# Local attention in a hybrid decoder layer: two halves of a block's values stored unadded, and summed by an adding load from GpSimd's queue

## The chip, the cores and the metric

The kernel runs on one NeuronCore of one Trainium2 chip. The metric is the device time of one execution in microseconds (us); lower is better. The engines are named as the profile names them: PE (TensorE, matrix products; PEld is its weight loads), DVE (VectorE), ACT (ScalarE), POOL (GpSimd) and SP (SyncE, which here only issues DMAs). Each engine executes its own instructions in the order in which they stand; semaphores hold an instruction back until what it needs is done. DMAs are moved by 16 DMA engines that all queues share.

## The reference

One layer of a decoder takes 1024 prompt tokens and 8 single-token samples through the same weights. A combined projection feeds three branches (a gated recurrence, a local attention, an attention over a memory); each is projected, gated and summed, then follow an output projection, a layer norm, a gated feed-forward and a second layer norm. What the change touches is the local attention of the prompt, in blocks of 128 tokens with a window of 128, 16 query heads in groups of 4 per key/value head, and the product of its output with the second branch weight:

```python
def swa_prompt(q, k, v, sinks):
    ...
    s = jnp.einsum('bnqkgd,bnmkd->bnkgqm', qb, kband).astype(jnp.float32) * scale
    ...
    p = sink_softmax(s, mask, sinks).astype(v.dtype)
    o = jnp.einsum('bnkgqm,bnmkd->bnqkgd', p, vband)
    return o.reshape(B, T, Q_W)
...
    merged = sum(gates[:, :, n] * (br @ w_branch[n]) for n, br in enumerate((a_out, s_out, c_out)))
    h = layer_norm(ALPHA * x + merged @ w_out, ln1_g, ln1_b)
```

All is float32. The kernel gets this precision from faster products by splitting an operand into a rounded part ("hi") and the rest ("lo"): three products, hi by hi, hi by lo and lo by hi, stand for one.

## The kernel before

The 1032 columns (1024 prompt tokens and 8 samples) are worked on in three chunks of 388, 386 and 258 (`CH`). Activations pass from stage to stage through buffers in DRAM, `scr_*`. The branches are projected in the order a, c, s (recurrence, memory, local attention). The products of a and c are "fill": a generator `jobs`, of which `fill(n)` takes n products of 24 matmuls each, so that PE has dense work while the attention's softmax runs on the other engines. The tile framework makes dependencies, places buffers and orders the instructions of each engine by its own estimates from the program's order, so an edit can move neighbours too.

**The window phase** (`windows`) runs over 4 key/value heads by 8 blocks, 32 in all. For each block `win_scores` makes scores on PE, adds the mask and takes a minimum on DVE, exponentiates on ACT, and normalises on DVE, POOL and ACT. One block later `win_values` transposes the probabilities on PE (tile `bt`), splits them (`bph` is rounded by ACT on L80, `bpl` is the rest by DVE on L81), and multiplies them by the values on PE (L613 and L614) into one bank `bo` of PSUM, 128 partitions by 512 columns. The values carry their own hi and lo part side by side in the 128 stationary columns, so partitions 0 to 63 of `bo` hold the product of one part, 64 to 127 that of the other, and the block's output is their sum. L616 to L622 make it, in two pieces of 256 columns: ACT copies partitions 64 to 127 to SBUF (L618, tile `bob`), DVE adds partitions 0 to 63 (L619), and SP stores the sum to `scr_s` (L621). `bob` has four buffers, two blocks' worth.

**The load of branch s** follows at once: `load_branch("s", 0)` before the last two fill products are finished, and chunks 1 and 2 inside `branch(2, "s")`. For each chunk and each of 8 rows k (128 channels each), SP loads the columns from `scr_s` into the tile `bsL` (L135), ACT rounds it into `bsH` and DVE subtracts it from `bsL` in place (L80, L81). For branch a's first two chunks the same line issues from POOL's queue. The products of branch s then come in the order m=0, m=1 for chunk 0, the same for chunks 1 and 2, and then m=2 to 7 (L114 to L116, tile `brs`). Each takes all 8 rows of its chunk in the order of k. DVE gates and sums the result (L652, L653, gate tile `gts`, loaded by SP on L669).

Of the kernel before, what the change touches and what calls it, by code (L numbers as in the profile page):

```python
# [10 lines left out]
F32 = mybir.dt.float32  # L11
F32R = mybir.dt.float32r
AF = mybir.ActivationFunctionType
ALU = mybir.AluOpType
# [4 lines left out]
P = 128  # L19
D = 1024  # L20
KT = D // P
TP = 1024
NB = 8
T = TP + NB
# [33 lines left out]
class Builder:  # L58
# [66 lines left out]
    def load_branch(self, br, c):  # L125

        act = self.act.setdefault(br, [[None] * 3 for _ in range(KT)])
        t0, n = CH[c]
        for k in range(KT):
            if br == "s":  # L130
                hi, lo = (self.slot(e, c, f"b{br}{e}{k}_{c}", 0) for e in "HL")
            else:
                hi, lo = self.hl(k, t0, n)
            queue = self.nc.gpsimd if br == "a" and c < 2 else self.nc.sync
            queue.dma_start(lo.bitcast(F32), self.scr[br][:, k, t0:t0 + n])  # L135
            self.split(hi, lo, lo.bitcast(F32))
            act[k][c] = (hi, lo)

# [462 lines left out]
    def win_values(self, kv, ops, b, pg):  # L601
        nc = self.nc
        nk, vs = len(range(max(b - 1, 0), b + 1)), ops[2]
        ov = self.bank("o", f"bo{kv}_{b}")
        for kk in range(nk):
            pt = self.bank("t", f"bt{kv}_{b}_{kk}")
            for g in range(4):
                nc.tensor.transpose(pt[:, g * P:(g + 1) * P], pg[g][:, kk * P:(kk + 1) * P], self.ident)
            hi = self.ph.tile([P, 512], F32R, tag="pt", name=f"bph{kv}_{b}_{kk}", bufs=4)
            lo = self.ph.tile([P, 512], F32R, tag="pt", name=f"bpl{kv}_{b}_{kk}", bufs=4)  # L610
            self.split(hi, lo, pt)
            v = vs[:, max(b - 1, 0) + kk, :]
            nc.tensor.matmul(ov, v, hi, start=kk == 0, stop=False)  # L613
            self.last_mm = nc.tensor.matmul(ov, v, lo, start=False, stop=kk == nk - 1).ins  # L614
        for i in range(2):
            ob = self.ph.tile([64, 256], F32, tag="ob", name=f"bob{kv}_{b}_{i}", bufs=4)  # L616
            o = ov[:, i * 256:(i + 1) * 256]
            nc.scalar.copy(ob, o[64:128, :])  # L618
            nc.vector.tensor_add(ob, o[0:64, :], ob)  # L619
            dst = self.scr["s"][:, 2 * kv + i, b * P:(b + 1) * P].rearrange("(e d) t -> d e t", e=2)  # L620
            nc.sync.dma_start(dst, ob.rearrange("p (e t) -> p e t", e=2))  # L621

    def windows(self, fill):

# [674 lines left out]
    def build(self):  # L1299
        nc, tc, io = self.nc, self.tc, self.io  # L1300
        self.setup()
        self.sums = 3
        self.sm = self.ctx.enter_context(tc.tile_pool(name="sm", bufs=4))
        shapes = {"c": [P, KT, T], "s": [P, KT, T], "a": [P, KT, T], "g": [P, 24, T], "xq": [P, KT, 2, TP],
                  "q": [P, KT, 2, TP], "k": [P, 2, 2, TP], "v": [P, 8, 512]}
        self.scr = {b: self.dram.tile(n, F32, name=f"scr_{b}") for b, n in shapes.items()}
        self.scf = [self.dram.tile([P, T], F32, name=f"scr_f{f}") for f in range(NF)]
        self.cdec = self.cst.tile([P, KT, NB], F32, name="cdec")
        pool = lambda name, side="left": tc.tile_pool(name=name, bufs=1, side=side, reuse_waits="tile")
        self.wpool = self.ctx.enter_context(pool("wpool"))  # L1310
        self.ctx.enter_context(pool("edge", "right")).tile([P, 8], F32, name="edge")
        with pool("tp", "right") as self.tp, pool("w1") as self.w1, pool("z") as self.z, pool("dp1") as self.dp:
            self.project()
        self.sums = 2
        self.act, self.merged = {}, [[None] * 3 for _ in range(KT)]
        with pool("acc") as self.acc:
            with pool("slots0", "right") as slots0:
                hy = ExitStack()
                tails = [hy.enter_context(pool("hy")), slots0]
                cut = CH[2][0]  # L1320
                self.HL = [([slots0.tile([P, cut], F32R, name=f"HL{k}{e}") for e in "hl"],
                            [tails[k // 4].tile([P, T - cut], F32R, name=f"HT{k}{e}") for e in "hl"]) for k in reversed(range(KT))][::-1]
                self.M = [self.acc.tile([P, T], F32, tag="acc", name=f"M{m}", bufs=8) for m in range(KT)]
                with ExitStack() as gp:
                    self.gp = gp.enter_context(pool("gp"))
                    jobs = chain(self.branch(0, "a"), self.branch(1, "c"))

                    def fill(n):
                        for _ in range(n):
                            next(jobs, None)  # L1330

                    with pool("ph1") as self.ph, pool("dp2") as self.dp:
                        self.mem_attention(fill)
                    with pool("ph2") as self.ph:
                        self.windows(fill)
                    late = ExitStack()
                    self.slots = [late.enter_context(pool("slots1", "right"))]
                    self.load_branch("s", 0)
                    fill(4)
                    for _ in self.branch(2, "s"):  # L1340
                        pass
                with pool("ph5") as self.ph:
                    self.out_proj(self.merged)
                    late.close()
                    self.tp = late.enter_context(pool("tp2", "right"))
                    self.w1 = late.enter_context(pool("ea", "right"))
                    direct = self.direct_units()
                    next(direct)
                with pool("cb") as self.cb:
                    next(direct)  # L1350
                    self.h_sums(1)
                    next(direct)
                    self.h_sums(2)
                    next(direct)
                    units = self.units()
                    next(units)
                    self.h_sums(6)
                hy.close()
                with pool("w2") as self.w2:
                    next(units)  # L1360
                late.close()
            with pool("ph6") as self.ph, pool("gd", "right") as self.gd:
                self.down()
# [146 lines left out]
```

## Time and profile before

| | |
|---|---|
| median of three runs | 1955.13 us (1952.33 to 1958.13) |
| the profiled execution | 1952.96 us, of which the span of the program is 1951.2 us |
| mean granted TensorE clock | 0.997 of full speed |
| window phase | about 840 to 1040 us of the span |
| load and first products of branch s | about 1041 to 1069 us |

Times in the profile are counted from the start of the span. In a row of groups stand the line, the engine, the operation, the tiles (output, arrow, inputs), the shape and the count; then the busy time, the mean of one instruction, and the idle time of the engine just ahead of them with what ended it. A tile's answer gives durations as minimum, median and maximum in ns. In a row of stretches, x is a count of instructions, PEclk the granted clock, and the DMA share the mean busy share of the 16 DMA engines (it can pass 1 a little, since packets overlap).

### The profile page before, as it was taken

The numbers are of one execution on the slowest core, as the hardware profiler recorded it, in microseconds if no ns is written. First come the engines' busy times: TensorE is split into PE (matmuls) and PEld (weight loads), VectorE is DVE, ScalarE is ACT, GpSimd is POOL, SyncE is SP. The second block draws the span as 40 slices with busy tenths as digits, with TensorE's granted clock in tenths as the row PEclk, the third lists the DMA queues.
The fourth block names the chain that finished last, engine by engine and source line by source line (L and its number), as shares of the span: only waits on it lengthen the run. The fifth ranks groups of instructions, "written<-read, shape, count | busy, mean of one in ns | idle before, by whom it ended". The sixth has DMA issues, their size and how long they took to land. (4 is left out here: it accounts for less than half of the span.)

```text
span 1951.2 us, 37943 instructions
## 1 busy us (share of the span) xinstructions
PE 1916.7 (98%) x14356; PEld 1887.1 (97%) x14356; DVE 1365.5 (70%) x2875; ACT 1015.2 (52%) x2198; POOL 139.3 (7%) x218
## 2 busy tenths in 40 slices
PE   8999999999999999999999999999999999999997
PEld 8999999999999999989999999999999999999997
DVE  8678987888777555389877557975565655747566
ACT  5455565456556446288775245643333333635445
POOL 1000000000011200011210000000000000402001
PEclk9999999999999999999999999999999999999999
DMA  7444555365323867567525241123222222846554
GB/s 231 149 163 151 169 170 180 126 207 171 130 90 135 278 212 226 153 173 210 163 74 176 94 145 43 47 71 98 77 87 87 88 82 73 284 127 187 154 155 143
DMA packets 170919, 281.92 MB, mean 144 GB/s; under 512 B 20864, under 2 KB 85456, under 8 KB 170704
## 3 DMA queue, kind: packets, MB, share of 16 engines
q1 hardware_dynamic: 165840, 264.70, 43.3%
q0 software_dynamic: 4896, 14.80, 2.3%
q8 instruction: 112, 1.84, 0.4%
q14 instruction: 71, 0.58, 0.1%
HBM read 214.64 MB, written 66.85 MB: 144 GB/s over the span
## 5 line engine op out<-in xcount | busy, mean ns | idle before, releaser
L1238 PE MATMUL dl<-gh,wd_l 128*128 128x388 f32 (+2 forms) x528 | 168.9, 321 | 2.1 <-DVE wd_l L81 2.1
L1236 PE MATMUL dl<-gh,wd_h 128*128 128x388 f32 (+2 forms) x528 | 168.8, 320 | 1.1 <-ACT gh L80 1.1
L1237 PE MATMUL dl<-gl,wd_h 128*128 128x388 f32 (+2 forms) x528 | 168.3, 319 | 0.0
L1238 PEld LDWEIGHTS dl<-gh,wd_l 128*128 128x128 f32 x528 | 99.5, 189 | 2.6 <-DVE wd_l L81 2.6
L1236 PEld LDWEIGHTS dl<-gh,wd_h 128*128 128x128 f32 x528 | 99.5, 189 | 1.3 <-ACT gh L80 1.3
L1237 PEld LDWEIGHTS dl<-gl,wd_h 128*128 128x128 f32 x528 | 99.8, 189 | 0.5 <-DVE gl L81 0.5
L1245 POOL DMA_DIRECT2D gl<-scr_f x66 | 35.5, 538 | 794.4 <-PE fb L1172 635.9
L80 ACT CAST u_1h<-us 128x512 fp32r<-128x512 f32 x48 | 29.8, 621 | 88.4 <-issue 43.5
L591 ACT ACTIVATE bp<-bp,bst 128x257 f32<-128x257 f32 (+1 forms) x128 | 62.7, 493 | 17.5 <-DVE bst L587 17.4
L80 ACT CAST u_2h<-us 128x512 fp32r<-128x512 f32 x48 | 29.7, 619 | 76.7 <-PE fb L1171 38.1
L283 DVE TENSOR_TENSOR us<-ur,ur 128x512 f32<-128x512 f32 x96 | 66.1, 688 | 4.2 <-DMA ur<-win 1.8
L283 DVE TENSOR_TENSOR us<-us,ur 128x512 f32<-128x512 f32 x96 | 66.3, 690 | 2.3
L81 DVE TENSOR_TENSOR u_6l<-ur,u_6h 128x512 fp32r<-128x512 f32 x48 | 33.8, 704 | 43.7 <-PE fb L1172 27.1
L114 PE MATMUL brs<-bsH,wbs_h 128*128 128x388 f32 (+2 forms) x192 | 61.4, 320 | 1.0 <-ACT bsH L80 1.0
L115 PE MATMUL brs<-bsL,wbs_h 128*128 128x388 f32 (+2 forms) x192 | 61.6, 321 | 0.0
L116 PE MATMUL brs<-bsH,wbs_l 128*128 128x388 f32 (+2 forms) x192 | 61.6, 321 | 0.0
L81 DVE TENSOR_TENSOR u_4l<-us,u_4h 128x512 fp32r<-128x512 f32 x48 | 33.1, 689 | 40.5 <-PE fb L1172 29.2
L587 DVE CUSTOM_DVE_ANT_0 bp<-bs,mask,nsnk 128x256 f32<-128x256 f32 (+1 forms) x128 | 54.5, 458 | 2.9 <-PE bs L584 2.2
L81 DVE TENSOR_TENSOR u_5l<-us,u_5h 128x512 fp32r<-128x512 f32 x48 | 33.1, 690 | 30.4 <-PE fd L1172 14.8
L1190 ACT ACTIVATE ft<-za 128x516 f32<-128x516 f32 x40 | 25.5, 637 | 52.3 <-DVE za L1189 52.3
L80 ACT CAST u_0h<-ur 128x512 fp32r<-128x512 f32 x48 | 29.8, 621 | 38.5 <-PE ub L300 20.6
L80 ACT CAST u_5h<-us 128x512 fp32r<-128x512 f32 x48 | 29.9, 623 | 38.2 <-DVE us L283 23.4
(2762 smaller groups left out, 8117.6 us busy)
## 6 DMA issues: line engine op xcount, KB each, us to landing
ur<-win SPq DMA_DIRECT2D x112, 256.0 KB
ur<-wgu SPq DMA_DIRECT2D x80, 256.0 KB
scr_f<-ft SPq DMA_DIRECT2D x40, 258.0 KB
dck<-cmk SPq DMA_DIRECT2D x32, 256.0 KB
dcv<-cmvT SPq DMA_DIRECT2D x32, 256.0 KB
st<-scr_q SPq DMA_DIRECT2D x32, 256.0 KB
scr_g<-za SPq DMA_DIRECT2D x10, 516.0 KB
scr_g<-zb SPq DMA_DIRECT2D x10, 516.0 KB
```

Of the source, the lines that this page charges most:

```text
L80: ins = self.nc.scalar.copy(hi, src).ins
L81: self.nc.vector.tensor_sub(lo, src, hi.bitcast(F32))
L114: nc.tensor.matmul(ps, sh, mh, start=i == 0, stop=False)
L115: nc.tensor.matmul(ps, sh, ml, start=False, stop=False)
L116: self.last_mm = nc.tensor.matmul(ps, sl, mh, start=False, stop=closes and i == last).ins
L283: nc.vector.tensor_add(src, a, b)
L587: nc.vector.tensor_tensor_reduce(pg[g], s[:, u * 256:u * 256 + n], msk, 1.0, snk[:, g:g + 1], ALU.add, ALU.min, st[:, g:g + 1])
L591: nc.scalar.activation(x, x, AF.Exp, bias=st[:, g:g + 1], scale=-1.0, accum_out=st[:, 4 + g:5 + g])
L1236: nc.tensor.matmul(ps, sh, mh, start=k == 0, stop=False)
L1237: nc.tensor.matmul(ps, sh, ml, start=False, stop=False)
L1238: self.last_mm = nc.tensor.matmul(ps, sl, mh, start=False, stop=closes and k == NF - 1).ins
L1245: self.nc.gpsimd.dma_start(lo.bitcast(F32), self.scf[f][:, t0:t0 + n])
```

## The change

The two halves are no longer added on DVE. ACT copies the whole bank `bo` at once, 128 partitions by 512 columns, and SP stores it in four pieces: partitions 0 to 63 to `scr_s`, 64 to 127 to a new DRAM buffer `scr_s2`. When branch s is loaded, a second DMA on POOL's queue reads the same columns of `scr_s2` and adds them to what stands in `bsL`. It covers the 1024 prompt columns; the 8 sample columns are in `scr_s` alone, so in the last chunk it takes 250 of 258.

```diff
@@ load_branch
             queue.dma_start(lo.bitcast(F32), self.scr[br][:, k, t0:t0 + n])
+            if br == "s":
+                held = min(n, TP - t0)
+                self.nc.gpsimd.dma_start(lo[:, :held].bitcast(F32), self.scr["s2"][:, k, t0:t0 + held],
+                                         accum_op=ALU.add)
             self.split(hi, lo, lo.bitcast(F32))
@@ win_values
-        for i in range(2):
-            ob = self.ph.tile([64, 256], F32, tag="ob", name=f"bob{kv}_{b}_{i}", bufs=4)
-            o = ov[:, i * 256:(i + 1) * 256]
-            nc.scalar.copy(ob, o[64:128, :])
-            nc.vector.tensor_add(ob, o[0:64, :], ob)
-            dst = self.scr["s"][:, 2 * kv + i, b * P:(b + 1) * P].rearrange("(e d) t -> d e t", e=2)
-            nc.sync.dma_start(dst, ob.rearrange("p (e t) -> p e t", e=2))
+        ob = self.ph.tile([P, 512], F32, tag="ob", name=f"bob{kv}_{b}", bufs=2)
+        nc.scalar.copy(ob, ov)
+        for e in range(2):
+            for i in range(2):
+                dst = self.scr["s" if e == 0 else "s2"][:, 2 * kv + i, b * P:(b + 1) * P]
+                nc.sync.dma_start(dst.rearrange("(e d) t -> d e t", e=2),
+                                  ob[64 * e:64 * e + 64, 256 * i:256 * i + 256].rearrange("p (e t) -> p e t", e=2))
@@ build
-        shapes = {"c": [P, KT, T], "s": [P, KT, T], "a": [P, KT, T], "g": [P, 24, T], "xq": [P, KT, 2, TP],
+        shapes = {"c": [P, KT, T], "s": [P, KT, T], "s2": [P, KT, TP], "a": [P, KT, T], "g": [P, 24, T], "xq": [P, KT, 2, TP],
```

The built programs show where the instructions stand. Lines of the change are four higher from `load_branch` on (L138 is the adding load, L620 the copy, L624 the store, L656 and L657 are L652 and L653 of before). First SP's queue at the end of the window phase, before: the stores of the last block and the loads of chunk 0.

```order
L621 DMA scr_s_73<-bob3_7_0_14001 64x2x128
L621 DMA scr_s_73<-bob3_7_1_14005 64x2x128
L135 DMA bsL0_0_14014<-scr_s_73 128x388
L135 DMA bsL1_0_14019<-scr_s_73 128x388
L135 DMA bsL2_0_14024<-scr_s_73 128x388
L135 DMA bsL3_0_14029<-scr_s_73 128x388
```

The same place of SP's queue in the change, as far as the gate and the first load of chunk 1:

```order
L624 DMA scr_s_73<-bob3_7_13940 64x2x128 x2
L624 DMA scr_s2_74<-bob3_7_13940 64x2x128 x2
L135 DMA bsL0_0_13951<-scr_s_73 128x388
L135 DMA bsL1_0_13957<-scr_s_73 128x388
L135 DMA bsL7_0_13993<-scr_s_73 128x388
L673 DMA gts1_14095<-scr_g_76 128x1032
L135 DMA bsL0_1_14139<-scr_s_73 128x386
```

Between `bsL1_0` and `bsL7_0` stand rows 2 to 6 of the same kind. Two stores of the last block have become four; the loads behind them keep their order.

Second, POOL's queue in the change at the same place (before, nothing stands on POOL between its last normalisation of the window phase and the loads of the last stage, which begin at 1663.1 us of the span):

```order
L602 TENSOR_SCALAR bp3_6_13713<-bp3_6_13713,bst3_6_13712 128x256
L602 TENSOR_SCALAR bp3_7_13795<-bp3_7_13795,bst3_7_13794 128x256
L138 DMA bsL0_0_13951<-scr_s2_74 128x388
L138 DMA bsL1_0_13957<-scr_s2_74 128x388
L138 DMA bsL2_0_13963<-scr_s2_74 128x388
L138 DMA bsL0_1_14139<-scr_s2_74 128x386
L138 DMA bsL0_2_14245<-scr_s2_74 128x250
```

All 24 adding loads stand there in the order of chunk and row (the rows between are alike). Each waits for the plain load of its tile.

Third, DVE at the start of branch s, before: the last products of branch c are gated, then the first operands are split.

```order
L652 SCALAR_TENSOR_TENSOR gtc7_13937<-gtc7_13937,brc7_2_14080 128x258
L81 TENSOR_TENSOR wbs11_l_14161<-wbs1r1__14158,wbs11_h_14160 128x512
L81 TENSOR_TENSOR bsL0_0_14014<-bsL0_0_14014,bsH0_0_14013 128x388
L81 TENSOR_TENSOR bsL1_0_14019<-bsL1_0_14019,bsH1_0_14018 128x388
L653 TENSOR_TENSOR M7_8972<-M7_8972,gtc7_13937 128x258
```

And in the change:

```order
L656 SCALAR_TENSOR_TENSOR gtc7_13876<-gtc7_13876,brc7_2_14025 128x258
L81 TENSOR_TENSOR wbs11_l_14106<-wbs1r1__14103,wbs11_h_14105 128x512
L657 TENSOR_TENSOR M7_8973<-M7_8973,gtc7_13876 128x258
L81 TENSOR_TENSOR bsL0_0_13951<-bsL0_0_13951,bsH0_0_13950 128x388
L81 TENSOR_TENSOR bsL1_0_13957<-bsL1_0_13957,bsH1_0_13956 128x388
```

The sum into `M` (L653, now L657), which frees the gate buffer that SP's next gate load waits for, has moved ahead of the first two splits of `bsL`.

## The prediction, made before the change was run

> **What bounds the kernel now.** I read the engine totals first, then stretches of time, then who waits for whom. The totals:
>
> ```profile
> span 1951.2 us, 37943 instructions
> PE 1916.7 (98%) x14356; PEld 1887.1 (97%) x14356; DVE 1365.5 (70%) x2875; ACT 1015.2 (52%) x2198; POOL 139.3 (7%) x218
> ```
>
> PE is busy for 98% of the span, so an edit to other engines can only matter where PE waits. All of PE's idle time is 1951.2 - 1916.7 = 34.5 us. Next the stretches that the change touches, five of the window phase and two of branch s (columns: stretch, then PE, PEld, DVE, ACT and POOL busy, clock, DMA share, GB/s):
>
> ```profile
> 840.00:880.00 40.00, 38.54 (x246) 34.33 (x245) 36.15 (x116) 38.74 (x120) 9.25 (x17) 1.00 0.63 175
> 880.00:920.00 40.00, 39.45 (x255) 36.75 (x254) 35.69 (x106) 33.24 (x98) 7.87 (x13) 1.00 0.78 217
> 920.00:960.00 40.00, 39.42 (x255) 36.58 (x255) 34.81 (x111) 31.17 (x96) 7.66 (x12) 1.00 0.63 175
> 960.00:1000.00 40.00, 39.45 (x257) 36.98 (x256) 31.91 (x99) 28.29 (x86) 7.54 (x12) 1.00 0.37 100
> 1000.00:1040.00 40.00, 39.68 (x255) 36.95 (x254) 29.92 (x83) 25.65 (x73) 6.24 (x8) 1.00 0.26 73
> 1045.00:1063.00 18.00, 17.58 (x97) 17.00 (x98) 15.75 (x35) 11.95 (x27) 0.00 (x0) 1.00 0.79 256
> 1063.00:1140.00 77.00, 77.00 (x498) 77.00 (x497) 44.53 (x94) 22.64 (x53) 0.00 (x0) 1.00 0.32 102
> ```
>
> In the 200 us of the window phase PE is idle for 1.46 + 0.55 + 0.58 + 0.55 + 0.32 = 3.46 us, though ACT is nearly full in the first 40 us and DVE is at 75 to 90% throughout. Behind 1063 us PE is idle for nothing: what is lost ahead of that point is paid in full at the end. The waits of PE and its weight loads from 830 to 1046 us:
>
> ```profile
> PEld bo L613 <- ACT bph L80: 7.8, 26, 0.6
> ...
> PEld bo L614 <- DVE bpl L81: 0.3, 1, 0.3
> ```
>
> The window phase waits for ACT's rounding of the probabilities, hardly for DVE; and weight loads can wait without PE standing still, since they run ahead of it.
>
> **What the change removes.** The rows of the window phase and, for the wide copy, one of the same shape in the memory attention:
>
> ```profile
> L619 DVE TENSOR_TENSOR bob<-bo,bob 64x256 f32<-64x256 f32 x64 | 26.5, 414 | 11.8 <-ACT bob L618 10.8
> ...
> L618 ACT COPY bob<-bo 64x256 f32<-64x256 f32 x64 | 23.4, 365 | 22.0 <-PE bo L614 18.2 <-DVE bob L619 1.8 <-DMA scr_s<-bob 1.4
> ...
> L521 ACT COPY cob<-co x16: 577/587/588, 716.3 to 812.6; 128x512 f32<-128x512 f32 x16
> ```
>
> DVE loses all 64 additions, 26.5 us. ACT exchanges 64 x 0.365 = 23.4 us for 32 x 0.587 = 18.8 us and gains 4.6 us, or 0.14 us a block, plus the 1.8 us in which it waited for DVE between the two copies. Nearly all of this lies beside PE's work. What can come back is PE's own idle time, 3.46 us at most; most of it follows a transpose that ACT cannot round sooner. I take 1.5 us, with 0 and 3.5 as ends. The scheduler also puts more fill between some transposes and their products; that is in the same range.
>
> **What it adds to the window phase.** There are 64 more stores of 64 KB:
>
> ```profile
> L621 SPq DMA_DIRECT2D scr_s<-bob x64: 574/580/1217, 844.5 to 1040.1; - x64
> ```
>
> That is 64 x 0.58 = 37 us of SP's queue. SP mostly waits for results there, and the DMA engines are 53% busy (the mean of the five shares). It costs nothing as long as ACT need not wait for a `bob` buffer: the old row shows 1.4 us of that in one place, behind a store two blocks old. If this cover went, each late store would hold ACT, and the next rounding behind it; I allow 1 us for it in the range.
>
> **What it adds to the load of branch s.** SP's queue at the boundary, then ACT and PE there:
>
> ```profile
> 1033.88 6.81 SPq L621 DMA_DIRECT2D scr_s<-bob  x4
> 1040.79 3.89 SPq L135 DMA_DIRECT2D bsL<-scr_s  x8
> 1046.81 0.32 SPq L669 DMA_DIRECT2D gts<-scr_g  x1
> 1047.23 9.32 SPq L135 DMA_DIRECT2D bsL<-scr_s  x16
> ```
>
> ```profile
> 1044.86 4.13 ACT L80 CAST bsH<-bsL 128x388 fp32r<-128x388 f32 x8
> ...
> 1060.05 0.41 ACT L80 CAST bsH<-bsL 128x258 fp32r<-128x258 f32 x1 [0.47 <-DMA bsL<-scr_s]
> ```
>
> ```profile
> 1045.42 0.62 PE L114 MATMUL brs<-bsH,wbs_h 128*128 128x388 f32 x2 [1.00 <-ACT bsH L80]
> ...
> 1065.46 0.29 PE L114 MATMUL brs<-bsH,wbs_h 128*128 128x258 f32 x1
> ```
>
> The last row is the first use of chunk 2's row 7, the last operand loaded. So the loads run from 1041 to 1060 us, and PE uses them from 1045.42 to 1065.46: five us of slack at the end and none at the start. Two terms follow.
>
> *The first operand.* The last bank is copied in one piece at 1038.42 us and is ready at 1039.01; four stores at 0.58 us occupy SP to 1041.3, so the loads start 0.6 us later. In the trace ACT began the first rounding as soon as it was free, at 1044.86, so the load had landed by then, 4.1 us after its issue. The adding load waits for that landing. Plain loads of this size from POOL's queue (of branch a, the answer on L135):
>
> ```profile
> L135 POOL DMA_DIRECT2D HL3l<-scr_a x2: 536/536/536, 637.3 to 645.3; - x2
> ...
> DMA to landing us min/median/max: 2.6/3.7/5.1
> ```
>
> They take 3.7 us from issue to landing, 2.6 at the shortest, by which the plain load of before could have landed at 1040.79 + 2.6 = 1043.4; between this and 1044.86 I take 1044. The first operand then stands at 1044 + 0.6 + 3.7 = 1048.3 us, ACT's 0.52 us later PE begins: 1048.8 instead of 1045.42, or **3.4 us** late. POOL has nothing queued behind the adding loads until the last stage, so only ACT, DVE and PE wait: ACT's later roundings, DVE's subtractions and the gating of `gts` stand behind them. SP's gate load does not, since the sum into `M` now stands ahead of the first split.
>
> *The bytes.* The 24 adding loads move 8 x 128 x 4 x (388 + 386 + 250) = 4.19 MB more. The DMA engines around the boundary:
>
> ```profile
> 1042.00:1048.00 6.00, 5.00 (x34) 4.49 (x33) 4.95 (x11) 4.07 (x9) 0.00 (x0) 1.00 0.87 270
> 1050.00:1054.00 4.00, 4.00 (x24) 4.00 (x24) 2.43 (x5) 1.89 (x4) 0.00 (x0) 1.00 1.05 363
> ```
>
> ```profile
> 1048.00:1050.00 2.00, 2.00 (x13) 2.00 (x12) 1.61 (x4) 0.99 (x2) 0.00 (x0) 1.00 0.87 275
> ...
> 1054.00:1058.00 4.00, 4.00 (x24) 3.72 (x23) 4.00 (x9) 3.79 (x10) 0.00 (x0) 1.00 0.92 271
> 1058.00:1062.00 4.00, 4.00 (x24) 4.00 (x23) 4.00 (x12) 2.50 (x8) 0.00 (x0) 1.00 0.47 150
> ```
>
> From 1042 to 1062 us the work is 6 x 0.87 + 2 x 0.87 + 4 x 1.05 + 4 x 0.92 + 4 x 0.47 = 16.7 us of all engines, Full engines move 363 GB/s at a share of 1.05, or 2.9 us a MB; the two weight loads of 256 KB behind the last load take 1.5 of the 16.7 us. One pass over the added bytes is 4.19 x 2.9 = 12.1 us. Starting at 1042.6 without a gap, the last load lands at 1042.6 + 15.2 + 12.1 = 1069.9 us; with 0.8 us for the rounding and the rest it is ready at 1070.7, 5.2 us after PE wanted it. That is the lower end. No row shows a DMA that adds. It must also read what stands in SBUF, so the upper end is a second pass: 1082.0 us, or 17.3 us late. The nearest row, the plain load from POOL's queue, reads once and writes once; adding makes two reads and a write, three halves of a pass in place of two. I take 1.5 passes, 18.2 us: ready at 1076.8, or **11.3 us** late. The first operand's delay is inside this, since PE's work of 20 us lies between them.
>
> The Trainium skill bears on this price. "Collectives: The Full Stack", under the bandwidth ceiling and the fold count, says of reduce-scatter that its addition in the DMA engine is free but needs two source reads through one read ring, and so halves the rate; by that rule the sum would have two passes, not 1.5, and end about 6 us later. No row here can decide it.
>
> **The sum.** On the profiled execution's own 1952.96 us (the span and 1.8 us around it): -1.5 + 11.3 = +9.8, or 1962.8, rounded to 1963 us. The median shown is 2.2 us above that execution; I leave the forecast on it and widen the range above.
>
> **Rivals.**
> *One pass.* The SBUF read costs the DMA engines nothing because the DRAM side limits them: -1.5 + 5.2 = +3.7, 1956.7 us. For it speaks that 363 GB/s is a rate from DRAM; against it that a share of 1.05 counts the engines as full.
> *Two passes or more.* Both reads go through the same side of each engine, and that side is the limit: -1.5 + 17.3 = +15.8, 1968.8 us. For it speaks that the share is already 1.05 under reads alone. (It is what the page named above would have.) A clock drop could come on top. The trace has one such place:
>
> ```profile
> 652.00:655.00 3.00, 0.49 (x2) 0.30 (x2) 1.20 (x3) 2.57 (x6) 0.00 (x0) 1.00 0.79 310
> 655.00:658.40 3.40, 3.40 (x11) 3.30 (x11) 3.40 (x10) 3.40 (x10) 0.00 (x0) 0.50 0.89 256
> ```
>
> After 2.5 idle us in three, PE ran for 3.4 us at half clock, which costs 1.7 us. A start 3.4 us late risks the same; I leave it out of the sum and in the range.
> *The window phase gives back more* (the other side). ACT is full from 840 to 880 us, and each rounding it makes sooner moves the weight load that waits for it; the 7.8 us of those waits are the most it can give. With one pass hidden in DMA idle time, so that only the first operand's 3.4 us remain, this is -4.4 or 1948.6 us. It decides once the window phase returns more than the load costs, 5.2 us at one pass. Against it: PE itself is idle for only 3.46 us there. That the additions stay somewhere is excluded: the built program has none on DVE.
>
> **Chances.** 1.25 to 1.75 passes, 0.36; about one pass, 0.27; two or more, 0.26; the window phase outweighs the load, 0.11. A measurement of this kernel tells about 0.3% from no change, 5.9 us. The first and third cases are slower by more, with a little of the second: 0.64. Most of the second and part of the last lie within: 0.29. Faster: 0.07. The range reaches from one pass with the window's 1.5 us, 1956, to two passes with the clock drop and the 2.2 us to the median, 1974; about 2 in 10 are left out, mostly below.
>
> **What would show it.** After: no L619 rows, ACT's copy at 0.59 us x 32, PE's idle time from 840 to 1040 us near 2 us. PE's first wait for `bsH` near 4.4 us. The DMA share full from 1043 to about 1076 us, where it now falls at 1060, with PE idle for about 12 us in all before chunk 2 is through. I am wrong if PE's idle time from 1044 to 1080 us is under 5 us (the adding load is cheap or hidden) or over 18 us (it costs more than two passes), or if the window phase moves by more than 3.5 us.

## The result, and the profile after

The change makes the kernel slower: 1985.19 us (median of 4 runs, 1984.08 to 1986.63) against 1956.32 us for the kernel before in the same session (4 runs, 1952.33 to 1958.13). The ratio is 1.015, with an interval of 1.0135 to 1.0165. The forecast was 1963 us with a range of 1956 to 1974: the direction was right, the size was not, and the time lies outside the range. The profiled execution took 1984.08 us, its span 1982.2 us, 31.0 us more than the span before.

First the engine totals of the change:

```profile
span 1982.2 us, 37869 instructions
...
PE 1931.6 (97%) x14356; PEld 1893.7 (96%) x14356; DVE 1342.9 (68%) x2811; ACT 1009.7 (51%) x2166; POOL 158.8 (8%) x242
```

DVE lost its 64 additions and is 22.6 us less busy, ACT 5.5 us less: what was to go, went. PE's busy time rose by 14.9 us although it does the same 14356 matmuls. Next the window phase in the stretches of before (columns as in the prediction):

```profile
840.00:880.00 40.00, 39.72 (x257) 36.15 (x256) 30.90 (x107) 36.23 (x113) 10.37 (x17) 1.00 0.53 138
880.00:920.00 40.00, 34.44 (x218) 30.23 (x218) 30.98 (x98) 33.24 (x97) 8.51 (x14) 1.00 0.81 226
920.00:960.00 40.00, 39.39 (x255) 37.76 (x254) 27.48 (x79) 25.13 (x71) 6.04 (x8) 1.00 0.66 178
960.00:1000.00 40.00, 39.06 (x252) 36.12 (x250) 27.70 (x87) 28.71 (x82) 6.33 (x11) 1.00 0.68 190
1000.00:1040.00 40.00, 39.99 (x259) 37.41 (x258) 27.05 (x80) 27.03 (x75) 7.39 (x10) 1.00 0.34 94
```

Four of the five stretches are as good as before or differ by 0.4 us at most, the first gained 1.2 us. All of the loss is in one stretch, 880 to 920 us: PE is idle there for 5.56 us instead of 0.55. SP's queue in that stretch, in the kernel before (start, duration, queue, line, DMA, count):

```profile
893.68 0.56 SPq L562 DMA_DIRECT2D vs<-scr_v  x1
896.57 0.62 SPq L621 DMA_DIRECT2D scr_s<-bob  x1
897.24 0.59 SPq L135 DMA_DIRECT2D HL0l<-scr_c  x1
...
901.62 0.38 SPq L135 DMA_DIRECT2D HL7l<-scr_c  x1
```

And in the change (the name scr_s stands for both buffers here, since numbers at the end of a name are left out):

```profile
897.49 2.57 SPq L624 DMA_DIRECT2D scr_s<-bob  x4
900.11 0.60 SPq L559 DMA_DIRECT2D ks<-scr_k  x1
900.76 1.23 SPq L563 DMA_DIRECT2D st<-scr_q  x2
904.23 2.58 SPq L624 DMA_DIRECT2D scr_s<-bob  x4
906.85 3.82 SPq L563 DMA_DIRECT2D st<-scr_q  x6
910.72 0.60 SPq L566 DMA_DIRECT2D vs<-scr_v  x1
911.36 0.82 SPq L135 DMA_DIRECT2D HL0l<-scr_c  x1
```

The loads of branch c's second chunk (`HL0l` to `HL7l`) leave 14 us later. They are the operands of the fill. Before, the first product with them began here:

```profile
902.43 0.34 PE L114 MATMUL brc<-HL0h,wbc_h 128*128 128x386 f32 x1
```

In the change PE has nothing but the windows' own short matmuls from 900.85 us until this row:

```profile
920.93 0.62 PE L114 MATMUL brc<-HL0h,wbc_h 128*128 128x386 f32 x2 [0.56 <-ACT HL0h L80]
```

The place of these loads in SP's order has moved too. Counted in the traces, they stood behind 21 of the 64 stores of the window phase before (the first of block 11), and stand behind 48 of the 128 in the change (the last of block 12). So of the 14 us about 7 pass until block 12's stores can begin, at 904.23 us, and about 7 are SP's own time for the entries from there to 911.32 us.

Then the load of branch s:

```profile
1040.00:1050.00 10.00, 9.91 (x65) 9.25 (x63) 4.18 (x8) 2.45 (x5) 0.00 (x0) 1.00 0.45 130
1050.00:1060.00 10.00, 2.25 (x5) 1.12 (x5) 2.43 (x5) 1.47 (x3) 4.49 (x5) 0.70 1.01 270
1060.00:1070.00 10.00, 7.42 (x15) 3.60 (x14) 2.25 (x4) 2.06 (x4) 3.51 (x4) 0.50 1.12 293
1070.00:1080.00 10.00, 9.21 (x31) 8.08 (x32) 4.78 (x9) 3.68 (x8) 5.29 (x6) 0.61 0.99 192
1080.00:1090.00 10.00, 9.56 (x51) 8.41 (x50) 5.20 (x11) 4.10 (x10) 7.06 (x8) 1.00 0.81 117
1090.00:1100.00 10.00, 9.31 (x54) 8.28 (x53) 8.24 (x18) 4.99 (x11) 0.87 (x1) 0.83 0.38 74
1100.00:1110.00 10.00, 10.00 (x65) 10.00 (x64) 4.68 (x10) 1.93 (x4) 0.00 (x0) 1.00 0.50 171
```

The counts tell more here than the busy time. From 1050 to 1100 us PE is idle for 12.25 us, but it does only 5 + 15 + 31 + 51 + 54 = 156 matmuls, which at the 65 of the last slice are 24 us of work: 26 us are lost. The other half of the loss is hidden in "busy": from 1060 to 1070 us, at a granted clock of 0.50, 15 matmuls are busy for 7.42 us, while the last slice does 65 in 10 us. The rest of the program is as before.

**PE's lag.** All runs below are read with one measure, worked out from the traces. Both programs have 14356 matmuls. I count them from the end, take the one that starts at a given time in the kernel before, and subtract the start times of matmuls with the same count. The lag at 846 us (of the kernel before) is what the execution lost ahead of the window phase, 846 to 1042 is the window phase, 1042 to 1080 the load, and 1080 to 1900 the rest. Within the load, chunk 0's first rows end at about 1050 (the change loses 18.3 us by then), and the last operand is used at 1065; behind it the change loses another 2.7 us by 1070. All in us:

| kernel | ahead | window phase | load of s | rest | median, ratio (interval) |
|---|---|---|---|---|---|
| the change | 0.7 | +4.8 | +24.9 | +0.3 | 1985.19, 1.015 (1.0135 to 1.0165) |
| e1_window | 4.8 | +3.3 | +0.1 | 0.0 | 1963.02, 1.0032 (1.002 to 1.0044) |
| e2_load | -0.2 | +0.1 | +25.1 | +1.7 | 1979.32, 1.0114 (1.0101 to 1.0127) |
| e3_plain | 3.7 | +4.1 | +4.1 | +3.4 | 1967.73, 1.0052 (1.0039 to 1.0065) |
| e4_ring | 5.0 | +3.6 | +18.5 | +3.5 | 1982.47, 1.0123 (1.0108 to 1.0137) |
| e5_narrow | 0.8 | +5.5 | +14.3 | 0.0 | 1974.09, 1.0087 (1.0066 to 1.0107) |
| e6_more_stores | 3.1 | +8.9 | +0.7 | 0.0 | 1966.05, 1.0043 (1.0028 to 1.0059) |
| e7_pool_store | 3.8 | -0.7 | +24.3 | +2.1 | 1983.99, 1.0139 (1.0118 to 1.016) |
| e8_dve_add | 1.4 | +4.3 | +8.9 | +1.5 | 1969.08, 1.0067 (1.0045 to 1.0089) |
| e9_wide | 5.5 | -0.6 | -0.1 | +0.1 | 1957.84, 1.0001 (0.999 to 1.0012) |
| e10_pool_ring | 0.0 | +0.4 | +18.5 | +1.9 | 1976.30, 1.0099 (1.0084 to 1.0115) |
| e11_pool_dve | -2.7 | -0.2 | +11.7 | +3.3 | 1970.16, 1.006 (1.0045 to 1.0076) |
| e12_warm | 2.9 | +6.1 | +27.2 | +1.6 | 1991.05, 1.017 (1.0153 to 1.0187) |
| e13_order | 1.0 | +3.8 | +29.7 | +3.6 | 1990.39, 1.0179 (1.0163 to 1.0194) |
| e14_narrow_ring | 4.8 | +3.5 | +9.7 | 0.0 | 1971.20, 1.0077 (1.0057 to 1.0097) |
| e15_all | 0.9 | +0.3 | +16.6 | +2.0 | 1973.56, 1.0094 (1.0077 to 1.0111) |

The first and the last column of lags lie in parts that the edits do not touch. They range over several us, so that a total alone says little below 5 us, and the verdicts below go by the lag of the stage. Each lag comes from one profiled execution. (In e12_warm its 99 additional matmuls are left out of the count.)

### The profile page after: what moved, and what is told of

Same layout as the page of the kernel before. It is cut to its first block, busy times and chain, and to the rows that moved or that the text cites. A ratio compares the mean times of both kernels' runs of the same rounds, so it can differ in the third digit from the quotient of the medians.

```text
span 1982.2 us, 37869 instructions
## 1 busy us (share of the span) xinstructions
PE 1931.6 (97%) x14356; PEld 1893.7 (96%) x14356; DVE 1342.9 (68%) x2811; ACT 1009.7 (51%) x2166; POOL 158.8 (8%) x242
## 5 line engine op out<-in xcount | busy, mean ns | idle before, releaser
L114 PE MATMUL brs<-bsH,wbs_h 128*128 128x388 f32 (+2 forms) x192 | 66.2, 345 | 11.8 <-ACT bsH L80 11.7
L80 ACT CAST u_2h<-us 128x512 fp32r<-128x512 f32 x48 | 29.7, 620 | 76.9 <-PE fb L1175 38.1
L115 PE MATMUL brs<-bsL,wbs_h 128*128 128x388 f32 (+2 forms) x192 | 66.3, 345 | 0.5 <-DVE bsL L81 0.2
L114 PEld LDWEIGHTS brs<-bsH,wbs_h 128*128 128x128 f32 x192 | 38.5, 201 | 16.7 <-ACT bsH L80 16.7
```

Source lines behind the costliest of these rows:

```text
L80: ins = self.nc.scalar.copy(hi, src).ins
L114: nc.tensor.matmul(ps, sh, mh, start=i == 0, stop=False)
L115: nc.tensor.matmul(ps, sh, ml, start=False, stop=False)
```

## The experiments

**e1_window and e2_load: the two halves of the change apart.** In e1 the adding load is taken out; in e2 it is put into the kernel before.

```diff
@@ e1_window, against the change
-            if br == "s":
-                held = min(n, TP - t0)
-                self.nc.gpsimd.dma_start(lo[:, :held].bitcast(F32), self.scr["s2"][:, k, t0:t0 + held],
-                                         accum_op=ALU.add)
@@ e2_load, against the kernel before
+            if br == "s":
+                held = min(n, TP - t0)
+                self.nc.gpsimd.dma_start(lo[:, :held].bitcast(F32), self.scr["a"][:, k, t0:t0 + held],
+                                         accum_op=ALU.add)
```

> The change without its adding load: branch s gets the first half alone (the second half is stored and left out). Theory W: the window phase loses by itself, since SP's queue now holds four stores of 0.6 us a block, and the loads of branch c's second chunk, which stood at 897 us before, leave at 911 us: about +5.5 us against the kernel before, near 1962 us, with PE idle for some 5 us from 900 to 920 us. Theory L (all of the loss is the adding load's, and the window phase only looks late in one profile): -1.5 us, near 1955 us. In both the first rounding of bsL starts as soon as ACT is free, and PE does not wait behind 1063 us.

> The kernel before, with the 24 adding loads alone: they add columns of scr_a, which has long been written, to bsL (branch s then gets another sum than the reference's). If the two parts of the change add up, this costs 28.9 - 5.5 = +23 us, near 1979 us, with adding loads 1.2 to 1.8 us apart and no more than three under way at a time. If the load is dear only because it starts late or because the stores of the second half stand ahead of it, the 1.5 passes of the prediction should hold: +11 us, near 1967 us.

The parts add up. The window phase alone lags by 3.3 us in its profile (the change: 4.8) and the load then costs nothing; the load alone lags by 25.1 us (24.9) and the window phase then costs nothing. So the dear load owes nothing to the late window phase, nor to the stores of the second half. e1's median of 1963.02 us agrees with theory W's 1962, though its profile has 4.8 us of lag ahead of the window phase that theory W does not explain.

**e3_plain: the same bytes without adding.**

```diff
-                self.nc.gpsimd.dma_start(lo[:, :held].bitcast(F32), self.scr["s2"][:, k, t0:t0 + held],
-                                         accum_op=ALU.add)
+                self.nc.gpsimd.dma_start(hi[:, :held].bitcast(F32), self.scr["s2"][:, k, t0:t0 + held])
```

> The change with its second load made plain: POOL still loads the same 4.19 MB of scr_s2, but into bsH, which ACT then overwrites; the second half is left out of the sum. Theory R (what is dear is the adding form: one packet per row, 0.88 us of POOL for each, three under way): the loads come down to 0.54 us of POOL each and to about 2.9 us a MB, so the loss is the window phase's 5.5 us and one pass, 5.2 us: near 1967 us. Theory B (bytes and contention, whatever the operation): within 4 us of the change, 1981 to 1989 us.

1967.73 us, where theory R had 1967: theory B falls. The load's lag is 4.1 us instead of 24.9, so 21 us of it hang on the adding form and on what comes with it. One such thing is the start: the plain load has a tile of its own and need not wait for the load from `scr_s`. In e3 the first ones leave here, 11 us before SP's first load of `bsL` (1049.44 us), and 14 of the 24 have left before it:

```profile
1038.04 1.68 POOL L138 DMA_DIRECT2D bsH<-scr_s  x3
```

In the change the first adding load leaves 3.2 us after SP's first (1050.37 and 1047.13 us). No run has plain loads that start as late, so how much of the 21 us the early start is worth stays open. POOL's queue in the page of the change, of e3 and of the kernel before (packets, MB, share of 16 engines):

```profile
q0 software_dynamic: 8352, 19.00, 3.7%
```

```profile
q0 software_dynamic: 6304, 19.00, 3.0%
```

```profile
q0 software_dynamic: 4896, 14.80, 2.3%
```

The same 4.20 MB go in 1408 packets plain and in 3456 adding. Summed over the trace's packet records, the plain packets take 12.25 us of all engines (the prediction's pass: 12.1), the adding ones 26.9 us: **2.2 passes** (25.0 us in e4, 28.0 in e2, so 2.0 to 2.3). A row of 1552 bytes takes 141 ns in the median when it adds and 66 ns when SP's queue loads it. In size this is near the rule quoted in the prediction from the Trainium skill, "Collectives: The Full Stack", bandwidth ceiling and fold count, by which two source reads halve the rate. That the second read is the reason is not shown by any run here.

**e4_ring: more adding loads under way.** POOL's queue in the change:

```profile
1050.37 1.86 POOL L138 DMA_DIRECT2D bsL<-scr_s  x2 [14.55 <-DMA bsL<-scr_s]
1052.57 0.89 POOL L138 DMA_DIRECT2D bsL<-scr_s  x1 [0.34 <-DMA bsL<-scr_s]
1057.21 0.87 POOL L138 DMA_DIRECT2D bsL<-scr_s  x1 [3.75 <-issue]
1059.08 0.87 POOL L138 DMA_DIRECT2D bsL<-scr_s  x1 [0.99 <-issue]
1060.71 0.86 POOL L138 DMA_DIRECT2D bsL<-scr_s  x1 [0.76 <-issue]
```

And ACT's roundings of the first three tiles, which start when these have landed:

```profile
1056.93 0.51 ACT L80 CAST bsH<-bsL 128x388 fp32r<-128x388 f32 x1 [6.48 <-DMA bsL<-scr_s]
1058.79 0.51 ACT L80 CAST bsH<-bsL 128x388 fp32r<-128x388 f32 x1 [1.35 <-DMA bsL<-scr_s]
1060.42 0.52 ACT L80 CAST bsH<-bsL 128x388 fp32r<-128x388 f32 x1 [1.11 <-DMA bsL<-scr_s]
```

After three issues POOL stands still, and each further issue comes 0.3 us after one landing: three are under way, no more. No semaphore holds POOL there; the profile calls it "issue".

```diff
-    nc = bacc.Bacc("TRN2", target_bir_lowering=False, num_devices=1, dynamic_dma_scratch_size=1024)
+    nc = bacc.Bacc("TRN2", target_bir_lowering=False, num_devices=1, dynamic_dma_scratch_size=1792)
```

> The change with 1792 in place of 1024 bytes a partition set aside for the descriptors of POOL's queue (L1499); nothing else. Theory R (the number of adding loads under way sets the pace: in the trace the fourth is issued 0.28 us after the first has landed, and so on): five under way in place of three, the distance between landings falls from 1.66 us towards POOL's own 0.9 to 1.2 us, so 24 x 0.46 to 24 x 0.7 = 11 to 17 us come back: 1968 to 1974 us. Theory T (the DMA engines themselves need 6.9 us a MB for adding packets): no change, 1982 to 1988 us.

The first six now go without a pause:

```profile
1053.81 5.47 POOL L138 DMA_DIRECT2D bsL<-scr_s  x6 [14.83 <-DMA bsL<-scr_s]
1061.45 0.87 POOL L138 DMA_DIRECT2D bsL<-scr_s  x1 [2.16 <-issue]
```

The time of the adding loads from issue to landing (the answer on L138), in the change and behind it in e4, and one stretch of e4:

```profile
DMA to landing us min/median/max: 3.1/4.3/7.8
```

```profile
DMA to landing us min/median/max: 4.6/8.5/11.4
```

```profile
1076.00:1088.00 12.00, 11.66 (x58) 11.08 (x57) 5.74 (x11) 4.45 (x10) 7.46 (x9) 0.89 1.16 238
```

The load's lag falls from 24.9 to 18.5 us, so the ring was worth 6.4 us. But theory R's 11 to 17 us do not come: each load takes 8.5 us in the median where it took 4.3, and the mean distance between landings falls only from 1.59 to 1.31 us (from the first landing to the last, 30.2 us instead of 36.6). The first ten landings are 1.6 us apart instead of 2.0, the others 1.1 instead of 1.3. Doubling the loads under way mostly makes them wait longer, since the DMA engines are now full to the end (a share of 1.16 from 1076 us, against 0.81 in the change's slice from 1080). By the total, 1982.47 us, theory T would have won outright; 7 us of lag in parts that the edit does not touch (5.0 ahead, 3.5 behind; the change has 0.7 and 0.3) cover most of the gain. Both theories hold in part: first the ring, then the price.

**e5_narrow and e14_narrow_ring: a quarter of the bytes.**

```diff
-                held = min(n, TP - t0)
+                held = 96
```

> The change with the 24 adding loads cut to 96 columns each (a quarter of the bytes, the same 128 rows; the other columns get the first half alone). Theory T (the adding packets' time in the DMA engines, which grows with their bytes: 141 ns at 1552 bytes and 102 at 1000, so about 58 at 384): 11 us of all engines in place of 24.6, and PE's lag over the load falls from 25 us to 9 to 12 us. Rival (a fixed cost of each adding load, POOL's 0.88 us and its wait for one of three under way): the loads stay 1.15 us apart or more and PE's lag stays above 18 us.

> The narrow adding loads (96 columns) with 1792 bytes a partition for POOL's descriptors. With 1024 bytes PE's lag over the load was 14.3 us, 13.7 of it by the end of chunk 0's rows. If that is the wait for one of three under way, five or six under way take it to 7 to 9 us. If it is the plain loads sharing the DMA engines, or POOL's 0.88 us for each, it stays at 12 us or more.

The packets of 384 bytes take 55 ns, as theory T had worked out (58), but the lag is 14.3 us, between the two. With the deeper ring it is 9.7 us, so 4.6 us of the 14.3 were the ring. In both, next to nothing is lost behind chunk 0's rows (0.6 us at most). What remains with the deeper ring is a start: the adding load cannot leave before the plain one has landed, and POOL needs 0.88 us for each, which keeps it busy for 19 of the 21 us from 1056.55 us. e14 came out above the 7 to 9 us expected for the ring alone.

The three sizes of adding packets also split their price. They take 55, 102 and 141 ns in the median at 384, 1000 and 1552 bytes, which is 0.074 ns a byte and some 27 ns a packet. Plain packets of SP's queue take 47 and 66 ns at 1032 and 1552 bytes, which is 0.037 ns a byte and some 9 ns a packet. By this estimate from the medians each byte costs twice as much when it is added, and most of what goes beyond two passes is the price of a packet.

**e6_more_stores and e7_pool_store: what holds up the window phase.** e6 is the kernel before with each store cut in two; e7 is the change with half of its stores on POOL's queue.

```diff
@@ e6_more_stores, against the kernel before
-            nc.sync.dma_start(dst, ob.rearrange("p (e t) -> p e t", e=2))
+            for e in range(2):
+                nc.sync.dma_start(dst[:, e, :], ob[:, e * P:(e + 1) * P])
@@ e7_pool_store, against the change
-                nc.sync.dma_start(dst.rearrange("(e d) t -> d e t", e=2),
+                (nc.gpsimd if e else nc.sync).dma_start(dst.rearrange("(e d) t -> d e t", e=2),
```

> The kernel before, with each store of bob cut in two (128 stores in place of 64, the same bytes; copies and additions as they were). Theory W (it is the number of stores on SP's queue that delays the loads of branch c): PE's work falls behind by 3 to 5 us between 880 and 925 us of the span and stays there, near 1960 to 1961 us. Rival (the wide copy on ACT or the missing additions on DVE change the order of the work): no lag, 1955 to 1958 us.

> The change with the stores of the second half issued from POOL's queue, so that SP again has two stores a block. Theory W: the lag of 4.8 us that PE has at the end of the window phase goes, and the 1.5 us of the prediction may come out as a gain; the load keeps its 25 us: 1978 to 1981 us. Rival (POOL, which holds the normalisation of a third of the probabilities, then waits for ACT's copy, and DVE and PE behind it): the window phase stays 4 us or more behind, 1984 us or above.

SP's queue in e6, and behind it in e7:

```profile
907.93 1.10 SPq L622 DMA_DIRECT2D scr_s<-bob  x2
909.77 1.18 SPq L622 DMA_DIRECT2D scr_s<-bob  x2
...
914.97 0.66 SPq L135 DMA_DIRECT2D HL0l<-scr_c  x1
```

```profile
900.05 1.28 SPq L624 DMA_DIRECT2D scr_s<-bob  x2
901.43 0.54 SPq L135 DMA_DIRECT2D HL0l<-scr_c  x1
```

With more stores and nothing else, the same loads leave at 914.97 us and PE falls 8.9 us behind, nearly all of it between 910 and 920 us: the place of theory W, and twice its size (why it is more than the 3.3 to 6.1 us of the other runs with four stores a block on SP was not tried). With two stores a block on SP, they leave at 901.43 us and the lag is gone, -0.7 us, although POOL waits for ACT's copies 21 times in 73.5 us. In e6 these loads stand behind 48 of 128 stores, as in the change, in e7 behind 22 of 64, near the 21 of before. The framework orders SP's entries anew in each build, so here the number of stores and the place of the loads go together; no run has four stores a block with the loads left in their place. e7's total (1983.99 us) is above the 1978 to 1981 expected; 3.8 us of its lag lie ahead of the window phase and 2.1 behind the load.

**e8_dve_add and e11_pool_dve: the sum on DVE.** The second half is loaded plain into `bsH` and added on DVE into a tile of its own (e8); e11 has the stores of e7 as well.

```diff
+                self.nc.gpsimd.dma_start(hi[:, :held].bitcast(F32), self.scr["s2"][:, k, t0:t0 + held])
...
+                src = self.slots[0].tile([P, CH[0][1]], F32, tag="sum", name=f"sum{k}_{c}", bufs=2)[:, :n]
+                if held < n:
+                    self.nc.vector.tensor_copy(src[:, held:], lo[:, held:].bitcast(F32))
+                self.nc.vector.tensor_add(src[:, :held], lo[:, :held].bitcast(F32), hi[:, :held].bitcast(F32))
+            self.split(hi, lo, src)
```

> The change with a plain second load from POOL's queue into bsH and an addition on DVE (into a tile of its own), 24 x about 0.55 us. All of the sum is computed. If the adding form is what is dear, the load costs the 4 us of the plain load and what DVE's 13 us more in some 25 us put on the path, 2 to 6 us: 1967 to 1973 us. If DVE becomes the bound there (it was busy for 8.6 of 10 us with the plain load alone), all 13 us show: 1975 to 1980 us.

> The addition on DVE at the load (all of the sum is computed), with the stores of the second half from POOL's queue. By PE's lag in the runs before: -0.6 us over the window phase and 8.9 us over the load, so 8.3 us behind the kernel before: 1964 to 1967 us. If the window phase still loses 4 us: 1969 us.

In e8 the load's lag is 8.9 us, 16 us less than with the adding load, and 4.8 more than with the plain load alone (its loads start early too, as in e3); 1969.08 us is in the range expected. e11's window phase is mended (-0.2), but its load lags by 11.7 us and the median of 1970.16 us misses the 1964 to 1967. Why its load is 2.8 us worse than e8's was not tried.

**e10_pool_ring, e13_order, e15_all: how much can be mended.** e10 has e7's stores and e4's ring. e13 is the change with the plain loads of chunks 1 and 2 on POOL's queue. e15 has all three.

```diff
@@ e13_order and e15_all, load_branch
-            queue = self.nc.gpsimd if br == "a" and c < 2 else self.nc.sync
+            queue = self.nc.gpsimd if br == "a" and c < 2 or br == "s" and c else self.nc.sync
             queue.dma_start(lo.bitcast(F32), self.scr[br][:, k, t0:t0 + n])
+            act[k][c] = (hi, lo)
+        for k in range(KT):
+            hi, lo = act[k][c]
             if br == "s":
...
-            act[k][c] = (hi, lo)
```

> The change with both repairs found so far: the stores of the second half from POOL's queue, and 1792 bytes a partition for the descriptors of POOL's queue. If the two add up, PE's lag is -0.6 us over the window phase and 18.5 us over the load: about 18 us in all, 1973 to 1977 us, and what is left is the adding packets' second pass. If POOL's stores hold its queue up as well (they fill the same descriptors), the load's lag is nearer 25 us: 1980 us.

> The change with the plain loads of chunks 1 and 2 moved from SP's to POOL's queue, four of chunk 1 ahead of chunk 0's adding loads and the others behind them. Theory Q (the adding loads of chunk 0 are late because the plain loads of later chunks, which SP issues at once, share the DMA engines with them): PE's lag over chunk 0's rows falls from 18.3 us to 9 to 12 us; the bytes come later, so the whole load's lag is 20 to 24 us. Rival (three adding loads under way, some 5 us each, whatever else runs): the lag over chunk 0 stays at 16 us or more, and the whole at 25 us or above.

> The change with everything that helped or may: stores of the second half from POOL's queue, 1792 bytes for its descriptors, plain loads of chunks 1 and 2 behind chunk 0's adding loads. Without the last edit PE's lag was 18.5 us over the load and 18.9 at its end. If the order of the loads is worth anything beside the deeper queue: 10 to 16 us of lag, 1968 to 1972 us. If not: 18 us or more, 1975 us or above.

e10 shows that the two repairs add up: +0.4 and +18.5 us, 1976.30 us as expected. In e13 the lag over chunk 0's rows falls from 18.3 to 14.3 us, between theory and rival, so the later chunks' plain loads account for some 4 us there; but the loads that were moved then come late themselves, the whole load lags by 29.7 us, and the edit alone is a loss. Beside the deeper ring it gives 1.9 us (16.6 against 18.5), and e15's 1973.56 us misses the 1968 to 1972.

**e12_warm: is the half clock a cost of its own?**

```diff
+        if br == "s" and m == 0:
+            ps = self.bank("mm", f"br{br}{m}_{c}")[:, :n]
+            idle = self.bank("t", f"idle{c}")[:, :n]
+            for k in range(KT):
+                for _ in range(30 if c == k == 0 else 3):
+                    nc.tensor.matmul(idle, wb[k][0], self.act["c"][7][c][0], start=True, stop=True)
```

> The change with matmuls that nobody reads put into PE's waits for bsH: 30 of 388 columns ahead of the first product of branch s and 3 ahead of each row of its m=0 products, about 5.3 us and 0.5 us a row. Theory C (the half clock that follows the waits costs time of its own): the granted clock stays at 1.00 from 1050 to 1100 us and the 2.7 us that PE loses behind the last operand come back, 1980 to 1983 us. Rival (the end is set by the last operand's landing alone): the clock is up, and the time stays within 1 us of the change, 1984 to 1986 us; should the clock account for much of the 25 us, it would fall below 1978 us.

```profile
1050.00:1060.00 10.00, 8.73 (x58) 8.41 (x56) 3.17 (x6) 1.25 (x2) 2.75 (x3) 1.00 0.88 242
1060.00:1070.00 10.00, 8.03 (x24) 6.24 (x24) 2.25 (x4) 2.43 (x5) 3.58 (x5) 0.66 1.11 287
1070.00:1080.00 10.00, 7.78 (x34) 5.99 (x35) 2.81 (x5) 2.57 (x6) 4.45 (x6) 1.00 1.06 240
```

The clock is higher (1.00, 0.66 and 1.00 where the change had 0.70, 0.50 and 0.61), yet the load's lag is 27.2 us instead of 24.9, and 18.7 instead of 18.3 over chunk 0's rows. So the half clock is not where most of the 25 us go: it runs while PE would wait anyway. The time of 1991.05 us is outside both expectations, but only 2.3 us of what this execution lags more than the change lie in the load; 4.8 lie in the other stages. Behind the last operand PE now loses 0.5 us instead of 2.7, with the clock at 1.00; but it comes to that operand 4.5 us later than in the change, counted from the start of the load, since the matmuls put in take PE's time. Whether the half clock alone costs those 2.7 us stays open.

**e9_wide: a version that might beat the kernel before.**

```diff
-        for i in range(2):
-            ob = self.ph.tile([64, 256], F32, tag="ob", name=f"bob{kv}_{b}_{i}", bufs=4)
...
+        ob = self.ph.tile([64, 512], F32, tag="ob", name=f"bob{kv}_{b}", bufs=2)
+        nc.scalar.copy(ob, ov[64:128, :])
+        nc.vector.tensor_add(ob, ov[0:64, :], ob)
```

> The kernel before with one copy and one addition of 64 x 512 a block in place of two of 64 x 256; the stores stay two. ACT gains about 32 x (2 x 0.365 - 0.587) = 4.6 us and DVE about as much; PE's own idle time in the window phase is 3.5 us. If ACT's rounding is what PE waits for, 1 to 2 us come back: 1954 to 1955 us. If PE's waits there have another cause, or the first store leaves later for the last block: within 1 us of the kernel before.

It saves ACT and DVE about 4.7 us each (32 copies of 584 ns and 32 additions of 682 ns) and PE 0.6 us of lag, which the total does not show: 1.0001 (0.999 to 1.0012). No version that was run beats the kernel before.

## Why the prediction was wrong

- **The removed work** was read rightly: ACT's copies take 584 ns x 32, no addition is left, and nearly all of it lay beside PE's work. The 1.5 us that were to come back are not shown: with the stores of the second half on POOL's queue (e7, e10, e11, e15) the lag over the window phase is -0.7, +0.4, -0.2 and +0.3 us, so about the 0 that was given as one end.
- **"It costs nothing as long as ACT need not wait for a `bob` buffer"** was the first step that failed. The step named the wrong dependent. SP's idle time and the 53% busy DMA engines did not matter; what stood behind the stores on SP's queue did, the loads of the next head and of branch c's second chunk, each behind a store that waits for a result, and now also a block and a half further back in SP's order. The window phase moved by +4.8 us instead of -1.5, which shows in e1, is made larger by e6 and undone by e7.
- **"I take 1.5 passes, 18.2 us"** was the second. The adding packets took 26.9 us, more than the upper end of two passes, 24.3. The step counted reads and writes alike, so that one read more made three halves of a pass; the packets show twice the time for each byte, and a higher price of the packet. With 26.9 us in place of 18.2, the prediction's own sum gives 1042.6 + 15.2 + 26.9 + 0.8 = 1085.5 us for the last operand, 20.0 us late instead of 11.3.
- **"Starting at 1042.6 without a gap"** was the third: with three adding loads under way the engines were not kept full (a share of 0.81 from 1080 to 1090 us). The run with the deeper ring lags by 18.5 us, near the 20.0 of the sum without a gap (18.1 with that run's own 25.0 us of packets), and the change by 24.9.
- **The first operand** was called 3.4 us late. The lag grew by 7.1 us before the first rows were through (5.5 to 12.6 us, at 1042 and 1046 us of the kernel before), since the first adding load, issued at 1050.37, let ACT begin only at 1056.93: over 6 us, and not the plain load's 3.7. In the full change this lies inside the bytes' delay, as the prediction had it; e14 shows it alone.
- **The bound on PE's idle time** (wrong if over 18 us) was a poor gauge. PE was idle for about 12 us, as forecast, but that is luck: 25 us were lost, and the other half stood as busy time, since lone matmuls at half clock count as busy for longer. Matmuls per slice would have been the gauge. The clock drop, left out of the sum, was seen, but e12 gives no sign that it is a large cost of its own.

The two-pass rival was the nearest of the cases and had a chance of 0.26 for its group; it was too low by the window phase (6 us), by the ring (6 us) and by the packets (some 2.6 us).

## What to carry to other kernels

Before an edit adds DMAs to an in-order queue, look up which loads stand behind them, in the order of the program as it is built with the edit, and what engine uses those as its filler; idle time of the queue is no cover when each of its entries waits for a result. An addition moved into a DMA is not free: the same bytes cost 2.2 times the engine time of a plain load here, and a plain load with the sum on DVE was 16 us cheaper, in part perhaps because a load into its own tile can start earlier. For work that PE waits for at the start of a stage, add on an engine that has the time and keep the load plain.

## What the runs showed of the hardware

- An adding load from POOL's queue went in one packet per row (144 packets for 128 rows, the small ones for signalling included), a plain one of the same rows in 59 on average, and POOL was busy for 0.88 us instead of 0.54 for each.
- With 1024 bytes a partition for the descriptors, three such loads were under way at a time; with 1792 the first six left without a pause. The wait shows as "issue" on POOL, with no releaser.
- More loads under way raised the median time to landing from 4.3 to 8.5 us while the mean distance between landings fell only from 1.59 to 1.31 us, with the DMA engines late in the load at a share of 1.16 where three under way had left them at 0.81.
